# RWKV in a four-layer trunk: keys, values and gates each projected in one piece, where keys and values went by halves

## The chip, the cores and the metric

The kernel runs on one core of a Trainium2 chip. The time is device time in microseconds (us) for one execution; the kernel before took 2302.71 us, the median of 3 runs (2301.54 to 2303.0). The profile shows one such execution by the hardware profiler, with TensorE as PE (its weight loads as PEld), VectorE as DVE, ScalarE as ACT, GpSimd as POOL and SyncE as SP.

## What is computed

A trunk of four residual layers on 256 tokens of 2048 channels. Layers 0 and 3 are RWKV time mixing, layer 1 is dilated attention, layer 2 is causal pooling. Only RWKV is touched by the change:

```python
xx = jnp.pad(h, ((0, 0), (1, 0), (0, 0)))[:, :S] - h
r, k, v, g = [(h + xx * mu[j]) @ w_in[j] for j in range(4)]
...
y = _rwkv7_scan(r, decay, k, v, -kk, kk * a)       # 32 heads of 64 channels
y = (group_norm(y) + bonus) * jax.nn.silu(g)
x = x + y @ w_out
```

Each of the four projections has its own mixed input `h + xx * mu[j]`, and each is a product of [256, 2048] with [2048, 2048]. In layer 3 the values are also blended with those of layer 0 by a low-rank sigmoid.

## The kernel before

**Projections.** `linear` forms a product by blocks of 256 output columns, each with 4 weight tiles of 512 rows. float32 is split into two parts (`whi`, `wlo` of the weights by L192 on ACT and L193 on DVE; `xhi`, `xlo` of the input by L169 and L170), and three matmuls stand for one product, all on L289. A block is 96 matmuls of 128x256. A matrix of 2048 columns has 8 blocks. I count blocks from the start of the program, 150 in all: in layer 0 the receptances are blocks 0 to 7, keys, values and gates 8 to 31, and the output projection 32 to 39. In layer 3 the same stand at 110 to 117, 118 to 141, and 142 to 149.

**Mixed inputs.** `mix` (L465) makes two of the 16 tiles of `h + xx * mu`: two loads `hl` of 256 KB from DRAM on SP's queue (L474) and two DVE operations (L478); `split` then adds one ACT and one DVE operation. The 8 pairs are made once per call of `part`, by `mixer_inputs`, and kept in SBUF while that call runs.

**Heads.** `heads` does the delta rule for one pair of channel tiles (four heads, 8 pairs per layer), beside the projections. Its stages are: decay, rate and normalized key, then scores (L723); an inverse of small blocks, stage D, whose matrices go through DRAM (`ntd`, `pxd`) around 30 short DVE operations (L765, L768), with `PX` (L782) and the products `q`, `zp`, `pp` on PE behind it (L791 to L816); stage C, four chunks of 64 tokens in a chain, `xps` (L842), `X` (L846), `ups` (L849), `UV` (L852, L853), `sps` (L857), the state `SV` (L860, L862), and the outputs `yps` (L867, L870); and stage E, the norm of the heads (`gps`, L882), the bonus (`bps`), the product with the gate (L898) and a store to `zd` (L899). The output projection reads `zd` back as `zl` (L407) and splits it. Stage C needs the centred values of its pair, which `take_v` stores (`vps` L592, `vcd`) when their block is done; D and C hold one pair each at a time, and at most three pairs are in flight (`FLY`).

**What sets the order.** `order` (L227) lists the calls of `part`. While `linear` emits a block, `tick` emits the steps of the heads that fall due, and a scheduler then fixes the order of the instructions on each engine. That order is static, and each engine runs its own in order. `drain` emits what is left of the heads after the last gate; the scheduler may still set matmuls of the output projection between them, as far as its inputs `zd` are there. Two PSUM tiles `lin` and three buffers of `whi` bound how far that goes: blocks 32 and 33 can each run up to the last two of their 16 input tiles before the last pair is done.

Of the kernel before, what the change touches and what calls it, by code (L numbers as in the profile page):

```python
# [16 lines left out]
D = 2048  # L17
# [12 lines left out]
ZMIN = -40.0  # L30
# [62 lines left out]
class Trunk:  # L93
# [68 lines left out]

    # ---------------------------------------------------------------- splits
    def split(self, src):
        """The two float32r parts of a pair of [128, 256] float32 tiles."""
        nc = self.nc
        hi = self.xp.tile([P, 2, S], F32R, tag="xhi", name="xhi", bufs=9)
        lo = self.xp.tile([P, 2, S], F32R, tag="xlo", name="xlo", bufs=9)
        nc.scalar.copy(hi, src)  # L169
        nc.vector.tensor_tensor(lo, src, hi.bitcast(F32), op=ALU.subtract)  # L170
        return hi, lo

    @staticmethod
    def once(make):
        """xs(k): the parts of tile k, made in pairs when first asked for."""
        made = {}

        def xs(k):
            if k // 2 not in made:
                made[k // 2] = make(k // 2 * 2)  # L180
            hi, lo = made[k // 2]
            return hi[:, k % 2], lo[:, k % 2]

        return xs
# [11 lines left out]
    def tick(self, us):  # L196
        """Trace the work beside the projections that falls due while these take `us` of TensorE.

        Its generators yield (TensorE time, delay of the next step) or (stage, condition)."""
        self.now += us  # L200
        self.load = max(0.0, self.load - us * self.RATE)
        slack = 0.0
        while True:
# [10 lines left out]
            it = min(due, key=lambda o: (o[1] != "C", o[3]))  # L214
# [7 lines left out]
            else:  # L222
# [3 lines left out]

    order = ((1, 0, D // 2, 1), (2, 0, D // 2, 2), (1, D // 2, D, 1), (2, D // 2, D, 1),  # L227
             (3, 0, D, 2))

# [10 lines left out]
    def linear(self, wv, n_lo, n_hi, xs, consume, kt=KT, tok_major=False, rounds=0,  # L240
               wide=False, then=None, blocks=None):
        """x @ w in columns n_lo..n_hi: out^T by 128 columns, or out by 256 columns.

        blocks: the first columns of blocks of 256, in place of n_lo..n_hi.
        then: (weights, first column, x, whole) of the next call, whose first tiles are made
        ahead; with whole, all the tiles of x during the last column."""
        nc = self.nc
# [53 lines left out]

    # ------------------------------------------------------------------ norm
    def sigmoid(self, out, z, bias=None, scale=1.0):
        """out = 1 / (1 + exp(-max(scale z + bias, ZMIN))), with exp and ln alone.

        bias: a column that holds the bias less ZMIN."""
        nc = self.nc
# [4 lines left out]
    def square(self, x, first, last, direct=False):  # L312
        """Adds a pair of tiles of x^T to the sums of squares of the tokens."""
        nc, sp = self.nc, self.sp
# [34 lines left out]
    def token_scales(self):  # L349
        """The norm's factors of the tokens along a row, and along a column the factors and  # L350
        eps over their squares."""
        nc = self.nc
# [15 lines left out]
    def norm(self, layer, xt):  # L368
        """h^T of a layer, one zero column ahead of it, from the pairs of tiles of x^T."""
        nc = self.nc  # L370
# [16 lines left out]
    def spill(self):  # L387
        """h^T and its token shift's difference to DRAM, for the later projections."""
        nc = self.nc
# [13 lines left out]
    def stored(self, li):  # L403
        """Split tiles of z^T from DRAM."""
        def load(k):
# [6 lines left out]
    def out_proj(self, wv, xs, kt, li):  # L412
        """x += z @ w_out, then the next layer's norm (or the output)."""
        nc = self.nc
# [47 lines left out]

    # ------------------------------------------------------------------ RWKV
    def mix(self, l, m, k):
        """Two tiles of h + (its token shift - h) mu_m."""  # L465
        nc = self.nc
# [34 lines left out]
    def lora_in(self, l, n, pool, w2, srcs):  # L501
        """The inner activations of the low-rank maps, [rank, 256] each, step by step."""
        nc, a = self.nc, self.i
# [29 lines left out]
    def lora_out(self, out, w2, j, src, rank, key):  # L533
        """max(w0 + src @ w2, ZMIN) - ZMIN of two tiles of 128 channels."""
        nc = self.nc
# [19 lines left out]
    def rwkv(self, l, li):  # L555
# [17 lines left out]
        def take_v(j, ps):  # L573
# [13 lines left out]
            def turn():  # L587
                # centred values by token, columns (head of a tile, tile, channel)
                vps = self.ps.tile([P, 2, 2, 2, C], F32, tag="ch", name="vps", bufs=2)
# [58 lines left out]
    def heads(self, l, li, pr, w2, srcs, have):  # L648
        """Four heads (two tiles of 128 channels) of the delta rule, from k^T to the normed output."""
        nc, sp = self.nc, self.sp  # L650
# [5 lines left out]
        j = 2 * pr  # L656
        # ---- decay, in-context rate
        sg = T("sg", [P, 4, S], 1)
# [18 lines left out]
        nc.vector.tensor_copy(Wc, W[:, :, :, C])  # L677
        # ---- normalized key, key of the state
        kk = T("kk", [P, 2, S], 1)
# [34 lines left out]
        yield "S", lambda: True  # L714
        # ---- scores
        mk = self.cst("smask")
        NT = T("NT", [P, 8, C], 2)
        MR = T("MR", [64, 2, 2, NC_, C], FLY)
        for q in range(2):
# [16 lines left out]
            yield 0.0, 1.0  # L736
        # ---- keys by token
        BT = T("BT", [P, 2, NC_, P], FLY)
# [6 lines left out]
        yield 0.9, 1.0  # L745
        # ---- (1 - N)^-1 of the diagonal blocks of 16, one block in a partition
        yield "D", lambda: True
# [29 lines left out]
        yield 0.0, 14.0  # L777
        # ---- blocks of 32, then 64
        rowm = self.cst("rows")
# [45 lines left out]
        yield "C", lambda: j in have[2]  # L825
        # ---- centred values by token
        UV = T("UV", [P, NC_, 2, 2, C], 1)
# [6 lines left out]
        for hh, rows in enumerate(half):  # L834
            nc.vector.memset(SV[rows, 0, hh], 0.0)
        # ---- chunks
        Y = T("Y", [P, 2, S], 1)
        each = [(q, hh, rows) for q in range(2) for hh, rows in enumerate(half)]
        for c in range(NC_):
# [33 lines left out]
            nc.scalar.copy(Y[:, :, c * C:(c + 1) * C], yps)  # L873
        # ---- norm of a head (its values have no mean), bonus
        yield "E", lambda: True
# [27 lines left out]

    # ------------------------------------------------------------- attention
    def rope_tables(self):
# [38 lines left out]
    def attention(self, li):  # L944
# [10 lines left out]
        nc.vector.memset(qkw[0:2 * ROPE_HALF], 1.0)  # L955
        # rope tables with the norm's weights in them: x1*c, x2*s, x1*s, x2*c
        tab = T("tab", [P, 6, 4, 2, ROPE_HALF], 1)
# [72 lines left out]
    def qk_heads(self, part, g, ps, tab):  # L1030
        """Norm and rotation of two heads of queries or keys."""
        nc, sp = self.nc, self.sp
# [26 lines left out]
    def attend(self, hd, ho, qkv, mask, oT):  # L1059
        """One head's softmax over the keys of all the dilations, step by step."""  # L1060
        nc, sp = self.nc, self.sp
# [49 lines left out]

    # --------------------------------------------------------------- pooling
    def pooling(self, li):
# [109 lines left out]
def host_layout(inputs):  # L1223
    g = {k: np.ascontiguousarray(v) for k, v in inputs.items()}
    arr = {n: g[n] for n in _PLAIN}
    for n in _BLOCKS:
        # blocks of 512 rows and 256 columns, each in one piece
        w = g[n]
# [51 lines left out]
```

## Time and profile before

| | |
|---|---|
| median of 3 runs | 2302.71 us |
| span of the profiled execution | 2307.1 us |
| PE busy / weight loads busy | 97% / 92% |
| DVE / ACT busy | 69% / 56% |
| blocks 8 to 33 of layer 0 (keys to the tail of the heads) | 133.3 to 638.3 us |
| blocks 118 to 143 of layer 3 (the same) | 1694.4 to 2233.9 us |

Matmuls overlap, so a busy PE may still wait: a wait shorter than one matmul's 0.28 us doesn't show as idle. The granted clock of PE has two levels, 2.4 GHz (1.00) and 1.2 GHz (0.50).

### The profile page before, as it was taken

What the parts mean: (1) busy time and instruction counts of PE and PEld (TensorE: products, weight loads), DVE (VectorE), ACT (ScalarE), POOL (GpSimd) and SP (SyncE); (2) the same over time, 40 slices, a digit from 0 to 9 for tenths busy, and PEclk for the clock granted to TensorE, in tenths of its full rate; (3) what the DMA queues carried; (4) which work ended last, traced back from release to release, by engine and by line L of the source; (5) the groups of instructions that cost most, each with busy time, mean ns of one, the idle gap of its engine ahead of it and who ended that gap; (6) DMA issues with size and microseconds to landing.
All of it is one profiled execution on the core that took longest, in us unless ns stands there. A gap on an engine that the chain in (4) does not pass through costs nothing.

```text
span 2307.1 us, 54751 instructions
## 1 busy us (share of the span) xinstructions
PE 2234.1 (97%) x22762; PEld 2119.4 (92%) x22762; DVE 1586.6 (69%) x2965; ACT 1301.4 (56%) x2074; POOL 4.7 (0%) x12
## 2 busy tenths in 40 slices
PE   7999999999999999999999999999999999999999
PEld 6998888889899999999999999998988888888889
DVE  7678788886556555555557675657678788887654
ACT  6557666665545444444456445546657666666542
POOL 0000000000000000000000000000000000000000
PEclk9999999999999999999999999999999999999999
DMA  7686777756576655454547567776586676665665
GB/s 265 226 259 187 236 212 214 230 155 187 197 249 189 179 151 175 151 177 149 179 150 251 177 183 220 246 220 227 177 282 188 205 230 191 203 194 170 198 212 159
DMA packets 217656, 464.38 MB, mean 201 GB/s; under 512 B 55488, under 2 KB 85824, under 8 KB 217408
## 3 DMA queue, kind: packets, MB, share of 16 engines
q1 hardware_dynamic: 199264, 432.92, 60.7%
q10 hardware_dynamic: 17504, 25.87, 3.2%
q8 instruction: 178, 2.92, 0.5%
q0 software_dynamic: 640, 2.10, 0.2%
q14 instruction: 70, 0.57, 0.1%
HBM read 410.47 MB, written 50.33 MB: 200 GB/s over the span
## 4 chain that ended last, share of the span: by engine, by line
PE 79%; DVE 11%; DMA 6%; ACT 3%; issue 2%; SPq 0%; DVEq 0%; POOL 0%; ACTq 0%; POOLq 0%
PE lin L289 65%; DVE wlo L193 3%; DMA hl<-hd 2%; PE u L515 1%; ACT whi L192 1%; PE yps L870 1%; PE ups L849 1%; DVE xlo L170 1%; PE xps L842 1%; PE q L791 1%; DMA kt<-kd 1%; PE sps L857 1%; PE z L540 1%; PE sc L723 1%; PE op L1106 1%
## 5 line engine op out<-in xcount | busy, mean ns | idle before, releaser
L289 PE MATMUL lin<-xhi,whi 128*128 128x256 f32 x3584 | 1057.5, 296 | 13.4 <-ACT xhi L169 13.2
L289 PE MATMUL lin<-xlo,whi 128*128 128x256 f32 x3584 | 1026.1, 287 | 8.3 <-DVE xlo L170 8.2
L193 DVE TENSOR_TENSOR wlo<-raw,whi 128x1024 fp32r<-128x1024 f32 x600 | 732.3, 1222 | 426.9 <-ACT whi L192 416.0
L289 PE MATMUL lin<-xhi,wlo 128*128 128x256 f32 x3584 | 1023.6, 286 | 0.7 <-DVE wlo L193 0.6
L192 ACT CAST whi<-raw 128x1024 fp32r<-128x1024 f32 x600 | 626.8, 1046 | 543.7 <-PE lin L289 500.1
L289 PEld LDWEIGHTS lin<-xhi,whi 128*128 128x128 f32 x3584 | 691.0, 193 | 36.9 <-ACT xhi L169 16.2
L289 PEld LDWEIGHTS lin<-xlo,whi 128*128 128x128 f32 x3584 | 692.5, 193 | 20.0 <-DVE xlo L170 11.5
L289 PEld LDWEIGHTS lin<-xhi,wlo 128*128 128x128 f32 x3584 | 691.9, 193 | 5.0 <-issue 1.9
L289 PE MATMUL lin<-whi,xhi 128*128 128x256 f32 x1152 | 332.4, 289 | 0.0
L289 PE MATMUL lin<-whi,xlo 128*128 128x256 f32 x1152 | 325.9, 283 | 0.0
L289 PE MATMUL lin<-wlo,xhi 128*128 128x256 f32 x1152 | 325.8, 283 | 0.0
L289 PEld LDWEIGHTS lin<-wlo,xhi 128*128 128x128 f32 x1152 | 221.0, 192 | 0.2
L289 PEld LDWEIGHTS lin<-whi,xhi 128*128 128x128 f32 x1152 | 220.9, 192 | 0.2
L289 PEld LDWEIGHTS lin<-whi,xlo 128*128 128x128 f32 x1152 | 220.8, 192 | 0.0
L478 DVE SCALAR_TENSOR_TENSOR mt<-hl,prm 128x256 f32<-128x256 f32 x152 | 71.2, 476 | 31.9 <-DMA hl<-hd 31.1
L169 ACT CAST xhi<-mt 128x512 fp32r<-128x512 f32 x96 | 58.8, 616 | 44.9 <-DVE mt L478 38.6
L170 DVE TENSOR_TENSOR xlo<-mt,xhi 128x512 fp32r<-128x512 f32 x96 | 65.2, 683 | 5.0 <-ACT xhi L169 4.5
L482 ACT ACTIVATE mt<-H,omm 128x256 f32<-128x256 f32 x120 | 54.2, 501 | 20.8 <-PE u L515 11.2
L484 DVE SCALAR_TENSOR_TENSOR mt<-H,prm,mt 128x256 f32<-128x256 f32 x120 | 52.8, 480 | 15.5 <-ACT mt L482 13.9
L765 DVE TENSOR_TENSOR tmp<-px,Nb 64x15 f32<-64x15 f32 (+7 forms) x240 | 46.7, 194 | 5.8 <-DMA Nb<-ntd 1.2
L768 DVE TENSOR_TENSOR px<-px,tmp 64x15 f32<-64x15 f32 (+7 forms) x240 | 46.8, 195 | 4.5
L723 PE MATMUL sc<-AR,BK 64*128 64x128 f32 x512 | 46.0, 295 | 0.5 <-DVE tmp L765 0.3
(229 smaller groups left out, 2231.6 us busy)
## 6 DMA issues: line engine op xcount, KB each, us to landing
raw<-in_a_w_in_dram SPq DMA_DIRECT2D x256, 512.0 KB, 4.3
raw<-in_b_w_in_dram SPq DMA_DIRECT2D x160, 512.0 KB, 3.5
hl<-hd SPq DMA_DIRECT2D x152, 256.0 KB, 4.5
raw<-in_a_w_out_dram SPq DMA_DIRECT2D x64, 512.0 KB, 4.2
raw<-in_c_w_in_dram SPq DMA_DIRECT2D x64, 512.0 KB, 3.6
raw<-in_c_w_out_dram SPq DMA_DIRECT2D x32, 512.0 KB, 4.2
raw<-in_b_w_out_dram SPq DMA_DIRECT2D x16, 512.0 KB, 4.7
zl<-zd SPq DMA_DIRECT2D x24, 256.0 KB, 4.2
```

What stands on the lines that cost most here:

```text
L169: nc.scalar.copy(hi, src)
L170: nc.vector.tensor_tensor(lo, src, hi.bitcast(F32), op=ALU.subtract)
L192: nc.scalar.copy(whi, raw)
L193: nc.vector.tensor_tensor(wlo, raw, whi.bitcast(F32), op=ALU.subtract)
L289: nc.tensor.matmul(ps[:, m], a, b, start=(k == 0 and m == 0 and q == 0), stop=(k == kt - 1 and q == 2), skip_group_check=True)
L478: nc.vector.scalar_tensor_tensor(t[:, q], h[q][:, 1], mu, h[q][:, 0], op0=ALU.mult, op1=ALU.add)
L482: nc.scalar.activation(t[:, q], self.H[:, k + q, 1:], AF.Copy, scale=self.omm[:, o:o + 1])
L484: nc.vector.scalar_tensor_tensor(t[:, q], self.H[:, k + q, 0:S], mu, t[:, q], op0=ALU.mult, op1=ALU.add)
L515: nc.tensor.matmul(u[:, tt], x[:, q, tt * P:(tt + 1) * P], wt[:, k + q], start=(k + q + tt == 0), stop=(k + q == KT - 1), skip_group_check ...
L723: nc.tensor.matmul(scs[hh][:, c], BK[rows, q, c], AR[rows, hh, q, c], start=True, stop=True)
L765: nc.vector.tensor_tensor(t, px[:, 0:i + 1, 0, i:i + 1].broadcast_to([64, i + 1, w]), Nb[:, i:i + 1, i + 1:].broadcast_to([64, i + 1, w]), ...
L768: nc.vector.tensor_tensor(dst, dst, t, op=ALU.add)
```

## The change

Keys are projected in one call of 8 blocks, then values in one, then gates. Before, the calls were keys 0 to 1023, values 0 to 1023, keys 1024 to 2047, values 1024 to 2047, gates. The last number of an entry, the rounds, is not read by `linear`. As each call makes its mixed input anew, there are now three mixings per RWKV layer in place of five. Apart from this the diff drops comments and docstrings only.

```diff
-    order = ((1, 0, D // 2, 1), (2, 0, D // 2, 2), (1, D // 2, D, 1), (2, D // 2, D, 1),
-             (3, 0, D, 2))
+    order = ((1, 0, D, 1), (2, 0, D, 2), (3, 0, D, 2))
```

The same instructions stand in another order. On PE, the first chunk of each pair of layer 0 stood before at blocks 14.1, 16.8, 19.2, 21.6, 24.1, 26.6, 28.8 and 31.4, and stands now at 17.6, 19.8, 22.3, 24.9, 27.4, 29.9, 32.0 and 32.9.

PE in layer 0 before, block 32.7 of the program, where the last pair's `gps` and `bps` stand (`lin` is a product of the output projection, `xhi_8553` an input tile of an earlier pair):

```order
L289 MATMUL lin_8702<-xhi_8509,wlo_8706 128x256
L289 MATMUL lin_8702<-xhi_8553,whi_8735 128x256
L289 MATMUL lin_8702<-xlo_8554,whi_8735 128x256
L289 MATMUL lin_8702<-xhi_8553,wlo_8736 128x256
L882 MATMUL gps_8683<-gsq_8679,c1_149 128x512
L884 MATMUL bps_8685<-kp_6683,c1_149 128x512
L289 MATMUL lin_8702<-xhi_8553,whi_8735 128x256
L289 MATMUL lin_8702<-xlo_8554,whi_8735 128x256
```

PE in layer 0 now, at block 33.75, the same place (line numbers are one less; `xhi_8625` is the last pair's own input tile, read back from DRAM):

```order
L841 MATMUL xps_8434<-SV_8361,AR_6949 64x64 x4
L848 MATMUL ups_8441<-X_8439,P_8355 64x64 x4
L856 MATMUL sps_8448<-UV_8360,BT_7578 64x64 x4
L866 MATMUL yps_8457<-AR_6949,SV_8361 64x64 x4
L869 MATMUL yps_8457<-MR_7339,UV_8360 64x64 x4
L841 MATMUL xps_8467<-SV_8361,AR_6949 64x64 x4
L848 MATMUL ups_8474<-X_8472,P_8355 64x64 x4
L866 MATMUL yps_8481<-AR_6949,SV_8361 64x64 x4
L869 MATMUL yps_8481<-MR_7339,UV_8360 64x64 x4
L881 MATMUL gps_8495<-gsq_8491,c1_149 128x512
L883 MATMUL bps_8497<-kp_6880,c1_149 128x512
L288 MATMUL lin_8514<-xhi_8625,whi_8547 128x256
```

Before, 93 matmuls of `lin` stood between `bps` and the first that reads the last pair's tile; now none does, and the last two chunks have none between their steps either (in layer 3: the last one).

DVE in layer 0 before, at block 12.5, where values began (`mt` is a mixed tile of the values' input, `tmp` and `px` belong to stage D of pair 0):

```order
L765 TENSOR_TENSOR tmp_2398<-px_2215,Nb_2210 64x15
L193 TENSOR_TENSOR wlo_2318<-raw_2315,whi_2317 128x1024
L768 TENSOR_TENSOR px_2215<-px_2215,tmp_2398 64x15
L170 TENSOR_TENSOR xlo_2360<-mt_2352,xhi_2359 128x512
L765 TENSOR_TENSOR tmp_2398<-px_2215,Nb_2210 64x28
L478 SCALAR_TENSOR_TENSOR mt_2381<-hl_2382,prm_151 128x256
L768 TENSOR_TENSOR px_2215<-px_2215,tmp_2398 64x2x14
L478 SCALAR_TENSOR_TENSOR mt_2381<-hl_2384,prm_151 128x256
```

DVE now at the same place, where keys go on with the input they have:

```order
L764 TENSOR_TENSOR tmp_2354<-px_2215,Nb_2210 64x15
L193 TENSOR_TENSOR wlo_2250<-raw_2247,whi_2249 128x1024
L767 TENSOR_TENSOR px_2215<-px_2215,tmp_2354 64x15
L193 TENSOR_TENSOR wlo_2296<-raw_2293,whi_2295 128x1024
L764 TENSOR_TENSOR tmp_2354<-px_2215,Nb_2210 64x28
L728 TENSOR_TENSOR MR_2278<-sc_2279,c1_149 64x256
L767 TENSOR_TENSOR px_2215<-px_2215,tmp_2354 64x2x14
L731 TENSOR_TENSOR AR_2198<-sc_2279,c1_149 64x512
```

The mixed tiles are gone from there, and the heads' own operations follow each other.

## Rows read from the trace of the kernel before

**Rows 1.** Busy time of the page: us, share of the span, instructions.

```profile
PE 2234.1 (97%) x22762; PEld 2119.4 (92%) x22762; DVE 1586.6 (69%) x2965; ACT 1301.4 (56%) x2074; POOL 4.7 (0%) x12
```

**Rows 2.** Stretches: from:to, length, busy (count) by engine, PEclk, DMA share, GB/s.

```profile
133.30:194.30 61.00, 57.24 (x447) 54.32 (x446) 45.08 (x68) 42.64 (x64) 0.00 (x0) 0.97 0.72 231
194.30:307.40 113.10, 102.97 (x1339) 91.68 (x1337) 94.98 (x226) 70.69 (x125) 0.00 (x0) 0.95 0.74 229
307.40:606.10 298.70, 294.72 (x4186) 261.63 (x4184) 235.93 (x556) 195.68 (x357) 0.00 (x0) 1.00 0.65 197
...
1757.60:1881.30 123.70, 113.81 (x1331) 99.72 (x1331) 100.45 (x231) 78.27 (x139) 0.00 (x0) 0.92 0.70 217
1881.30:2196.30 315.00, 303.50 (x4187) 267.66 (x4186) 245.19 (x571) 204.24 (x371) 0.00 (x0) 0.98 0.63 192
```

**Rows 3.** Stretches again, L289 alone on PE, at each level of the clock.

```profile
649.80:695.90 46.10, 46.10 (x387) 46.10 (x386) 1.00 0.71 220
...
1578.90:1582.30 3.40, 3.33 (x15) 3.33 (x16) 0.50 0.99 332
```

**Rows 4.** Page's groups of mixing: count | busy us, mean ns; and its loads.

```profile
L478 DVE SCALAR_TENSOR_TENSOR mt<-hl,prm 128x256 f32<-128x256 f32 x152 | 71.2, 476 | 31.9 <-DMA hl<-hd 31.1
L170 DVE TENSOR_TENSOR xlo<-mt,xhi 128x512 fp32r<-128x512 f32 x96 | 65.2, 683 | 5.0 <-ACT xhi L169 4.5
...
hl<-hd SPq DMA_DIRECT2D x152, 256.0 KB, 4.5
```

**Rows 5.** Waits of PE, blocks 12 to 16 and 122 to 126: us, times, longest.

```profile
PE lin L289 <- DVE xlo L170: 2.9, 4, 1.5
...
PE lin L289 <- DVE xlo L170: 3.4, 4, 1.3
PE xps L842 <- DMA SV<-vcd: 3.1, 1, 3.1
PE lin L289 <- ACT xhi L169: 1.8, 3, 0.9
```

**Rows 6.** Timeline, last pair of layer 0: start, length, engine, line, operation.

```profile
621.98 1.04 PE L882 MATMUL gps<-gsq,c 128*128 128x512 f32 x2
623.31 0.68 PE L289 MATMUL lin<-xhi,whi 128*128 128x256 f32 x1
...
626.96 0.33 SPq L899 DMA_DIRECT2D zd<-Y  x1
...
632.47 0.62 ACT L169 CAST xhi<-zl 128x512 fp32r<-128x512 f32 x1 [0.81 <-DMA zl<-zd]
...
633.14 0.51 PE L289 MATMUL lin<-xhi,whi 128*128 128x256 f32 x2 [0.29 <-ACT xhi L169]
```

**Rows 7.** Timeline, last pair of layer 3, the same ends.

```profile
2217.60 1.04 PE L882 MATMUL gps<-gsq,c 128*128 128x512 f32 x2
...
2230.46 0.50 PE L289 MATMUL lin<-xhi,whi 128*128 128x256 f32 x2 [1.13 <-ACT xhi L169]
```

**Rows 8.** Timeline, steps of a chunk in layer 0's last pair.

```profile
595.22 0.45 PE L842 MATMUL xps<-SV,AR 128*64 128x64 f32 x8
595.72 0.27 ACT L846 COPY X<-xps 128x128 f32<-128x128 f32 x1 [0.69 <-PE xps L842]
...
614.29 0.39 PE L857 MATMUL sps<-UV,BT 128*64 128x64 f32 x5
615.41 0.60 DVE L862 TENSOR_TENSOR SV<-SV,Wc 64x128 f32<-64x128 f32 x2
618.07 0.45 PE L849 MATMUL ups<-X,P 64*64 64x64 f32 x8
618.95 0.26 ACT L853 COPY UV<-ups 64x128 f32<-64x128 f32 x1 [1.44 <-DVE UV L852]
```

**Rows 9.** Timeline, stage D of layer 0's last pair, from its last DVE step on.

```profile
552.77 0.18 DVE L768 TENSOR_TENSOR px<-px,tmp 64x15 f32<-64x15 f32 x1
...
566.37 0.91 ACT L782 ACTIVATE PX<-pc,c 128x256 f32<-128x256 f32 x2
```

## The prediction

> **What bounds the kernel now.** I read the page's busy times first. PE is busy 97% of the span and its weight loads 92%, DVE 69% [rows 1], so outside of short places the time is PE's work. The change leaves PE the same instructions. So the question is only where PE waits, and at which clock it works, before and after. Next I read a quiet stretch of L289 alone: four blocks, 384 matmuls, in 46.1 us, that is 0.12 us for one; with the granted clock at 0.50, 15 to 16 in 3.40 us, some 0.21 us [rows 3]. Time at the low level thus loses 1 - 0.12/0.21 = 0.44 of itself.
>
> Then I cut layer 0's scan by blocks, and layer 3's like it [rows 2]. The reader is to take length less PE's busy time as its idle time, and twice (1 less the granted clock) times the length as time at the low level.
> - Blocks 12 to 16 (values by their first half, start of the second half of keys): layer 0, 113.1 us, idle 10.1, low level 11.3 us, so 5.0 lost by it. Blocks 122 to 126 in layer 3: 123.7 us, idle 9.9, low level 19.8, so 8.7 lost. Together 33.7 us in ten blocks.
> - Blocks 17 to 31, and 127 to 141: 298.7 and 315.0 us, idle 4.0 and 11.5, low level about 0 and 12.6 (5.5 lost). 21 us in thirty blocks.
> - Blocks 8 to 11 have keys with stage A of two pairs, and are the same after: 61.0 us, idle 3.8.
>
> So the waits are densest where the halves change over. The waits there have names [rows 5]: PE on the split input tiles, 2.9 in layer 0 and 3.4 + 1.8 in layer 3, is 8.1 us of mixing itself; the 3.1 us on SV is the heads' own.
>
> Last I read the end of the scan, since the heads end later now. In layer 0 the last pair's `gps` starts at 621.98, its result is stored at 626.96, its tile read back is split at 632.47, and the first matmul that reads it starts at 633.14: 11.2 us. In layer 3 it is 2217.60 to 2230.46: 12.9 us. PE waited only 0.29 and 1.13 us of that, as 93 matmuls of the output projection (11.2 us) stood between [rows 6, 7].
>
> **The change part by part.**
>
> *Two mixings less per layer.* For each, 8 pairs with two DVE operations of 0.476 and one of 0.683, 13.1 us; two of them in two layers are 52 us of DVE, and 64 loads of 256 KB less on SP's queue [rows 4]. None of that is PE's time; it pays only as waits that go. Floor: the 8.1 us by name. Ceiling in those ten blocks: all 33.7. In the new order four of the five blocks hold keys alone, since the heads stop at three pairs in flight until values come; I expect them to wait like blocks 8 to 11 do, some 4 us per layer, so 33.7 - 8 = 26 us gained. The heads' work that is no longer there isn't gained, it is moved behind.
>
> *Blocks 17 to 33.* One mixing (for gates) stands there still, in place of three; values' own is made in block 16. But the stages C and E of all pairs lie there now, and SV's load comes 36 projection matmuls after `vps`, so layer 0 may wait on it as layer 3 did (3.1). The named waits on mixing there are near nothing, so I take a gain of 2 us in both layers, with ends of -10 (the idle time per block as now, over two more blocks, and the SV wait twice) and +10 (half of the 21).
>
> *The end of the heads.* In the order, no matmul of the output projection is left between `bps` and the first that reads the last pair's tile, in either layer: blocks 32 and 33 have run to their 14th input tile. So the way from `gps` to that tile is bare: 11.2 and 12.9 less some 1.3 us for `gps` and `bps` themselves (621.98 to 623.31), less the 0.29 and 1.13 waited already: 20.1 us in both layers [rows 6, 7]. Ends: 18 and 24, since the two layers differ by 1.7 us already.
>
> *The last chunks, bare.* From `xps` to the end of X 0.77 us, from `ups` to the end of UV 1.14, from `sps` to the end of SV 1.72: 3.6 us, in which PE works 5 steps of 0.45, so 1.4 us of waiting per chunk without cover [rows 8]. The last chunk has no `sps`, so 0.6, and then the copy of Y and its square, 1.1 us. I take 3 us per layer, 6; ends 3 and 10.
>
> *Stage D of the last pair.* From its last DVE step to the start of PX passed 13.4 us (552.95 to 566.37), then 0.9 for PX [rows 9], all behind projections. In the new order some 57 projection matmuls (6.9 us) and two chunks and the norm of pair 6 (about 5 us by the steps of rows 8 and the 1.3 of `gps` and `bps`) stand between that step and the first product `q`. So about 2 us is bare, and some 1 us in the products behind it, which have few projections between them. 3 us per layer, 6; ends 0 and 28 (all of it bare).
>
> *The clock.* The stretch at 1578.90, at 0.50, stands where layer 3 begins, behind the norm that PE waits for [rows 3]. A bare end of 10 us and a sparse PE ahead of it should do the same, for one to two such stretches: 0.44 of 3.4 to 10 us, 1.5 to 4.5 per layer. I take 3, so 6.
>
> *More changes between kinds of matmul.* PE's order goes from `lin` to something else 171 and 189 times in the two scans, 157 and 178 before. Where a small matmul follows `lin`, the start comes some 0.1 us later than another `lin` would, and going back costs as much: 25 times 0.2 us is 5 at most; I take 4.
>
> Sum: -26 - 2 + 20 + 6 + 6 + 6 + 4 = +14 us. The profiled span is 2307.1 us, so 2321 on that scale; it lies 4.4 above the median, 2302.71, which gives 2317.
>
> On whether less DVE work pays at all, stretch and span differ: over the span DVE is far behind PE, yet in blocks 12 to 16 it is busy 95.0 of 113.1 us, and the weight loads 91.7 [rows 1, 2]. The Trainium skill (Perfetto Trace Analysis, Identifying the Most-Contended Engine) says to optimize the engine with the highest occupancy first, with the weight loads as PE's measure. Read over the whole span it gives the 26 + 2 us no place; read by stretch it lets DVE count there.
>
> **The rivals.**
>
> *Faster: waits fall by more than I count, from stage to stage.* Waits shorter than 0.28 us don't show as idle, and each one that is removed also spares time at the low clock. If all 33.7 us and another 10 of the middle go, against the low ends at the tail (18 + 3 + 0 + 3 + 2 = 26), the sum is -18: 2285; I put the middle of this case at -12, 2291. It decides from the point where the ten blocks give back more than the 42 us that I charge the end. For it: 52 us of DVE time and 16.8 MB of loads are really gone. Against it: only 8.1 us of PE's waits bear the name of mixing.
>
> *No change.* The same gain meets a cheaper end; within 5 us either side of 2303.
>
> *Much slower: the last pair's stage D is bare.* If its round trip through DRAM isn't covered, 14 us per layer stand in place of 3: +22, 2339. It decides from the point where pair 6's chunks end before the inverse is back. For it: in layer 3 fewer projections (48) stand before `q`. Against it: DMA is busy 0.65 of the time in the middle [rows 2] and will have less to move.
>
> *DVE's relief gives nothing.* PE is the bound in every stretch, so the gain is 0 and the end costs its 42: 2345. The waits on `xlo` and `xhi` speak against it [rows 5]. The rule of the Trainium skill named above (Perfetto Trace Analysis, Identifying the Most-Contended Engine), read over the whole span, is this case.
>
> *The change doesn't do what it says:* the order shows that it does, in both layers.
>
> **How the numbers follow.** Forecast 2317, with its own range 2308 to 2330 from the ends of the single terms: 0.50. Faster, at 2291: 0.20. No change: 0.13. Stage D bare: 0.11. No relief: 0.06. A difference under 0.2%, 4.6 us, can't be told from none. The forecast's share lies above that, so slower is 0.50 + 0.11 + 0.06 = 0.67, same 0.13, faster 0.20. The range of 8 in 10 goes from 2293, inside the faster case, to 2341, past the bare stage D.
>
> **What would show it.** In the new profile: PE idle for 9 to 13 us in each RWKV layer right before the first L288 that reads the last pair's tile, released by ACT L169 after `zl`, and the granted clock at 0.50 behind it; blocks 12 to 16 shorter by far, some 70 us, with the granted clock near 1.00 and no named wait on `xlo`; L477 88 times in place of 152; the blocks from 17 on longer. If PE waits at the end for less than 5 us, the step on the bare way is wrong; if blocks 12 to 16 still hold 10 us of idle time, the step on mixing is. If the middle shows 20 us more or less idle time than now, the whole sum is wrong in its sign or its size.

## The result: 2.4% slower, four times the forecast's loss

| us | before | after |
|---|---|---|
| median beside each other (4 runs each) | 2302.86 | 2360.41 (2353.61 to 2369.87) |
| ratio, 95% interval | | 1.024 (1.0208 to 1.0271) |
| the profiled execution's span | 2307.1 | 2351.7 |
| time at the low level of TensorE's clock in it | 68 | 117 |
| the changed kernel again, on another chip | 2308.70 | 2357.39, 1.0191 (1.0153 to 1.0229) |

The forecast was 2317, from 2293 to 2341. The sign was right, the size was not: 43 us are missing, and the time lies outside the range.

The page of the changed kernel: busy time by engine, beside [rows 1], and its group and loads of mixing, beside [rows 4]:

```profile
PE 2265.1 (96%) x22762; PEld 2136.3 (91%) x22762; DVE 1547.3 (66%) x2869; ACT 1287.5 (55%) x2042; POOL 4.7 (0%) x12
...
L477 DVE SCALAR_TENSOR_TENSOR mt<-hl,prm 128x256 f32<-128x256 f32 x88 | 41.0, 480 | 23.5 <-DMA hl<-hd 23.3
...
hl<-hd SPq DMA_DIRECT2D x88, 256.0 KB, 4.7
```

The relief is there as announced: PE has the same 22762 matmuls, DVE 96 operations and SP 64 loads less. Yet PE's busy time is 31 us longer. No matmul was added, so what grew is the time of some of them. The clock was at its low level 49 us longer; at the prediction's price of 0.44 that is some 22 of the 31 us. Where the other 9 come from is not shown.

The scans by blocks, as in [rows 2] (length, busy time and count of PE, PEld, DVE, ACT, POOL, granted clock, DMA share, GB/s). The rows of each layer are blocks 8 to 11, 12 to 16, 17 to 31, and 32 and 33; in layer 3 the same from 118 on:

```profile
132.70:194.20 61.50, 57.59 (x446) 54.25 (x445) 45.11 (x68) 41.87 (x62) 0.00 (x0) 0.97 0.70 227
194.20:270.60 76.40, 70.55 (x789) 67.36 (x788) 58.55 (x130) 44.52 (x67) 0.00 (x0) 0.98 0.66 214
270.60:590.00 319.40, 314.39 (x4277) 275.10 (x4275) 237.79 (x544) 206.29 (x374) 0.00 (x0) 0.99 0.60 181
590.00:668.30 78.30, 63.07 (x755) 49.69 (x754) 33.16 (x91) 26.24 (x54) 0.00 (x0) 0.80 0.38 124
1724.30:1788.10 63.80, 58.69 (x447) 55.15 (x446) 45.46 (x68) 41.94 (x62) 0.00 (x0) 0.95 0.69 218
1788.10:1864.00 75.90, 72.15 (x793) 68.08 (x791) 59.02 (x130) 45.96 (x71) 0.00 (x0) 0.98 0.68 216
1864.00:2204.50 340.50, 331.37 (x4305) 287.02 (x4303) 253.19 (x573) 222.25 (x404) 0.00 (x0) 0.96 0.60 178
2204.50:2278.50 74.00, 61.21 (x754) 49.25 (x753) 33.43 (x86) 25.10 (x52) 0.00 (x0) 0.86 0.38 125
```

And the same two last rows of the kernel before, which do not stand ahead of the prediction:

```profile
606.10:638.30 32.20, 31.91 (x297) 28.52 (x294) 19.19 (x32) 17.44 (x30) 0.00 (x0) 1.00 0.60 205
2196.30:2233.90 37.60, 36.25 (x334) 31.21 (x333) 19.42 (x35) 17.17 (x29) 0.00 (x0) 1.00 0.53 182
```

Blocks 12 to 16 are shorter by 37 and 48 us, but they also hold some 550 matmuls less. Most of those stand in blocks 32 and 33 now (755 in place of 297, 754 in place of 334), which are longer by 46 and 36 us and hold 28 us of idle time at a clock of 0.80 and 0.86. Outside the two scans the two executions agree: span less the scans is 1262.6 us before and 1261.9 after. So the 44.6 us lie in the scans.

With the prediction's two measures (idle time, and 0.44 of the time at the low level) these rows give:

| part, both layers, us | before | after | difference | forecast |
|---|---|---|---|---|
| blocks 12 to 16: idle + clock | 20.0 + 13.7 | 9.6 + 2.7 | -21 | -26 |
| blocks 17 to 31: idle + clock | 15.5 + 5.5 | 14.1 + 14.8 | +8 | -2 |
| blocks 32 and 33: idle + clock | 1.6 + 0 | 28.0 + 22.9 | +49 | +38 |
| the rest of 44.6, not told apart (forecast: changes between kinds of matmul) | | | +9 | +4 |

The end of layer 0's scan in the changed kernel, line by line, beside [rows 6], and the same matmuls of layer 3, beside [rows 7] (start, length, engine, line, operation, idle time before it and its releaser):

```profile
651.43 2.08 PE L881 MATMUL gps<-gsq,c 128*128 128x512 f32 x2 [1.01 <-ACT gsq L877]
653.30 1.91 PE L883 MATMUL bps<-kp,c 128*128 128x512 f32 x2
...
658.31 0.33 SPq L898 DMA_DIRECT2D zd<-Y  x1
...
662.99 0.62 ACT L169 CAST xhi<-zl 128x512 fp32r<-128x512 f32 x1 [8.10 <-DMA zl<-zd]
...
663.66 0.80 PE L288 MATMUL lin<-xhi,whi 128*128 128x256 f32 x2 [8.44 <-ACT xhi L169]
...
2262.64 1.12 PE L881 MATMUL gps<-gsq,c 128*128 128x512 f32 x2 [1.02 <-ACT gsq L877]
...
2273.26 0.79 PE L288 MATMUL lin<-xhi,whi 128*128 128x256 f32 x2 [8.63 <-ACT xhi L169]
```

The way from `gps` to the last tile takes 12.2 and 10.6 us, and PE stands idle for 8.4 and 8.6 of them: the bare end is where the prediction put it. What it did not see is around it. Layer 0's tail in pieces:

```profile
616.00:626.00 10.00, 6.01 (x246) 5.12 (x246) 4.19 (x7) 3.57 (x6) 0.00 (x0) 1.00 0.56 186
626.00:640.00 14.00, 14.00 (x125) 11.66 (x120) 3.62 (x9) 3.48 (x8) 0.00 (x0) 0.51 0.13 40
640.00:650.00 10.00, 8.22 (x117) 6.37 (x113) 4.28 (x12) 2.90 (x8) 0.00 (x0) 1.00 0.18 55
650.00:667.00 17.00, 7.54 (x24) 4.52 (x23) 3.65 (x7) 2.91 (x6) 0.00 (x0) 0.50 0.31 93
```

From 626 to 640 PE has no idle time at all, and yet its granted clock is 0.51: it fell at 626.0, behind ten microseconds in which PE worked 6.0. It is low a second time from 650 to 667. That is 31 us at the low level in one tail, and 51 in both layers together.

### The profile page after: what moved, and what is told of

It is laid out like the page before. It is cut to its first block, busy times and chain, and to the rows that moved or that the text cites. A ratio compares the mean times of both kernels' runs of the same rounds, so it can differ in the third digit from the quotient of the medians.

```text
span 2351.7 us, 54546 instructions
## 1 busy us (share of the span) xinstructions
PE 2265.1 (96%) x22762; PEld 2136.3 (91%) x22762; DVE 1547.3 (66%) x2869; ACT 1287.5 (55%) x2042; POOL 4.7 (0%) x12
## 5 line engine op out<-in xcount | busy, mean ns | idle before, releaser
L481 ACT ACTIVATE mt<-H,omm 128x256 f32<-128x256 f32 x120 | 54.1, 501 | 20.5 <-PE u L514 12.1
L851 DVE COPY UV<-ups 64x128 f32<-64x128 f32 x64 | 18.0, 281 | 61.6 <-PE ups L848 60.7
L169 ACT CAST xhi<-mt 128x512 fp32r<-128x512 f32 x64 | 39.4, 616 | 33.1 <-DVE mt L477 27.4
L477 DVE SCALAR_TENSOR_TENSOR mt<-hl,prm 128x256 f32<-128x256 f32 x88 | 41.0, 480 | 23.5 <-DMA hl<-hd 23.3
L859 DVE TENSOR_TENSOR SV<-SV,sps 64x128 f32<-64x128 f32 x96 | 27.3, 284 | 33.4 <-PE sps L856 31.6
```

What stands on the lines that cost most here:

```text
L477: nc.vector.scalar_tensor_tensor(t[:, q], h[q][:, 1], mu, h[q][:, 0], op0=ALU.mult, op1=ALU.add)
L481: nc.scalar.activation(t[:, q], self.H[:, k + q, 1:], AF.Copy, scale=self.omm[:, o:o + 1])
L859: nc.vector.tensor_tensor(SV[rows, c + 1, hh], SV[rows, c, hh], sps[rows], op=ALU.add)
```

## The experiments

All ratios are to the kernel before, run on the same chip in the same comparison (medians 2307.5, 2308.7, 2307.8 and 2307.2 us). Differences in us are the ratio's.

### Is it mixing? Three mixings in the old order, five in the new

`three`: the order by halves, but the second halves make no new mixed input (the second half of the keys is computed from the values' one).

```diff
-                    then = (win(m2), lo2, self.mixer_inputs(l, m2), False)
+                    then = (win(m2), lo2, xs if n in (1, 2) else self.mixer_inputs(l, m2), False)
```

> The order of before, but only three mixings per RWKV layer: the second halves of keys and of values are projected from the mixed input that the first half of the values made (so the second half of the keys is computed from the wrong mixed input; the count and order of the projections are before's, 64 loads of 256 KB and 52 us of DVE are gone). If the mixings themselves were what PE waited for in blocks 12 to 16 (theory: mixing), the time falls by 20 to 30 us against before, to some 2275 to 2283. If those waits were the heads' own, which only moved (rival: heads), it falls by less than 8, to 2295 to 2303.

Measured: 2294.86 us, 0.994 (0.9917 to 0.9962), -13 us. Its blocks 12 to 16 and 122 to 126, beside the second and fourth line of [rows 2]:

```profile
196.20:305.20 109.00, 101.75 (x1338) 90.70 (x1336) 89.85 (x223) 67.70 (x118) 0.00 (x0) 0.97 0.68 208
...
1755.50:1874.50 119.00, 111.55 (x1331) 97.99 (x1330) 95.80 (x233) 74.93 (x133) 0.00 (x0) 0.93 0.64 200
```

With the heads left where they were, two mixings less per layer shorten these stretches by 4.1 and 4.7 us, not by 13 each as the forecast's 26 would have it. Idle time there is 14.7 us in place of 20.0. This does not show that the other waits are the heads' own, for the two mixings don't lie wholly in these blocks: of the 55 operations L478 that the kernel before has in the ten blocks, `three` keeps 32, and waits on split input tiles of 5.4 us, of 8.1, are left. What the run does bound is the worth of both mixings over the whole kernel, 13 us.

`remix`: the new order with five mixings (keys and values in two calls each, at the same places).

```diff
-    order = ((1, 0, D, 1), (2, 0, D, 2), (3, 0, D, 2))
+    order = ((1, 0, D // 2, 1), (1, D // 2, D, 1), (2, 0, D // 2, 2), (2, D // 2, D, 1),
+             (3, 0, D, 2))
```

> The changed order (all keys, all values, gates), but with five mixings as before: the calls are keys 0 to 1023, keys 1024 to 2047, values 0 to 1023, values 1024 to 2047, gates, so each half makes its input anew. PE's order is that of the changed kernel. Theory mixing: 20 to 26 us slower than the changed kernel, 2380 to 2386. Rival heads: blocks 12 to 16 are so light now that the two mixings are covered, 0 to 8 us slower, 2360 to 2368.

Measured: 2372.26 us, 1.0294 (1.0242 to 1.0347), +68. That is 12 us above the changed kernel's 1.024, and 24 above its 1.0191; the intervals overlap in the first case. The mixings are thus worth 13 us in the old order and 12 or 24 in the new one, by the first or the second time of the changed kernel; moving the projections alone costs 68.

### Is it the bare end? Cut it short, fill it, or make one in the old order

`direct`: the changed kernel, with the last pair's gated output kept in SBUF, without its store and load.

```diff
-            dma(self.zd[li % 2][j // 2], Y)
+            if j == KT - 2:
+                self.zlast = self.mp.tile([P, 2, S], F32, tag="mt", name="zlast", bufs=2)
...
+            if k == KT - 2 and self.zlast is not None:
+                t, self.zlast = self.zlast, None
+                return self.split(t)
```

> The changed kernel, but the last pair's gated output stays in SBUF and is split from there; its store to DRAM and the load of it back are left out, nothing else. Theory: the end of the heads is bare, so what is taken from its chain comes off the time: store and load were 5.5 us in layer 0 and 7 in layer 3 before, so 11 to 13 us faster than the changed kernel, 2347 to 2350, and some of the time at the low clock with it. Rival (something else ends last there, or the loss lies in the middle): within 4 us of 2360.

Measured: 2355.23 us, 1.0214 (1.018 to 1.0248). Less than the 11 to 13 us expected, and not told apart from the changed kernel's 1.024 and 1.0191. PE's longest wait at the end of layer 0 in it (lines are one or more further, by the edit), and the stretch:

```profile
PE lin L289 <- ACT xhi L170: 3.7, 1, 3.7
```

```profile
597.30:674.40 77.10, 66.18 (x757) 52.53 (x754) 33.81 (x90) 26.55 (x54) 0.00 (x0) 0.78 0.36 120
```

The wait fell from 8.4 to 3.7 us, yet the two blocks take 77.1 us in place of 78.3: the clock there is 0.78 in place of 0.80, so 3 us more at the low level. Taking away the wait did not take away what surrounds it. From the last `gps` to the end of the scan pass 11.9 and 12.1 us in place of 15.9 and 15.3, so some 7 us in both layers were saved there; a gain of that size lies within the intervals, and the run can neither show nor exclude it.

`dummy`: the changed kernel with eight useless 128x512 matmuls put into that wait.

```diff
+        if j == KT - 2:
+            dps = self.ps.tile([P, 2, S], F32, tag="ch", name="dps", bufs=2)
+            for _ in range(8):
+                nc.tensor.matmul(fl(dps), self.cst("bd"), fl(sq), start=True, stop=True)
```

> The changed kernel with useless work added: eight matmuls of 128x512 into a spare PSUM tile, from the last pair's reciprocal norms, in the bare wait at the end of each RWKV layer's heads (some 7 us of PE that would idle). Theory clock: the granted clock is at 0.50 when the projection goes on because PE idled, so the useless work makes the kernel 2 to 6 us faster, and the low stretch behind the wait is gone from the clock's records. Rival: the low clock there comes from the sparse chunks ahead or costs nothing: within 2 us, or up to 2 us slower.

Measured: 2358.74 us, 1.0211 (1.0184 to 1.0238), again the changed kernel's time. PE's idle time at the end of layer 0 falls to 7.8 us, but the clock was already low when the filling began:

```profile
595.10:676.40 81.30, 73.53 (x771) 55.55 (x770) 32.91 (x89) 26.11 (x54) 0.00 (x0) 0.79 0.35 118
...
631.30:665.20 33.90, 31.67 (x245) 24.00 (x242) 8.86 (x23) 8.58 (x20) 0.00 (x0) 0.50 0.11 33
665.40:676.40 11.00, 9.64 (x40) 5.52 (x39) 3.47 (x8) 1.88 (x3) 0.00 (x0) 1.00 0.44 143
```

The useless matmuls start at 664.1, so the low level was there before the wait that they fill. Behind them it is gone: the clock is high again from 665.3 on, where the changed kernel's projection still ran at 0.50 for some 3 us behind its wait (663.7 to 667). Neither shows in the time of the whole kernel, so the run does not separate the wait from the clock.

`bare`: the kernel before, but the RWKV output projections read their input tiles from the last to the first, so that nothing covers the heads' end. One index stayed as it was, so a tile meets another tile's weights of its group of four; number, shape and order of instructions are as described.

```diff
+            kcs = list(range(kt // 4))[::-1 if rev else 1]
...
+                k = kc * 4 + (3 - k4 if rev else k4)
...
+        self.linear(wv, 0, D, xs, consume, kt=kt, then=then, rev=self.layers[li] % 3 == 0)
```

> The kernel before, five mixings and its order of columns; only the output projections of the two RWKV layers read their sixteen input tiles from the last to the first, so that none of their matmuls can stand before the last pair of heads is done. Nothing of the heads or of mixing changes, nothing is left out. Theory end (what the change costs is that the heads' last steps lose the output projection's matmuls that covered them): in the kernel before, from the start of the output projection to the first matmul on the last pair's tile pass 27 us in layer 0 (606.1 to 633.1) and 34 in layer 3 (2196.3 to 2230.5), during which some 15 to 17 us of heads' matmuls stand; PE waits the rest, 10 to 17 us per layer, later steps lose their cover as well, and the low level follows: +25 to +55 us, ratio 1.011 to 1.024. Rival (the end costs little, as the heads run faster with PE to themselves, and the loss of the change comes from the middle): 0 to +10 us, ratio at most 1.004. The low level's time rises from 68 to over 100 us by the first, stays under 80 by the rival.

Measured: 2342.02 us, 1.0131 (1.0103 to 1.016), +30, inside the first theory's range. PE's wait for the last tile in layer 0 and in layer 3 (the projection is L292 here), and blocks 17 to 31 of layer 0, which end with it:

```profile
PE lin L292 <- ACT xhi L169: 8.6, 1, 8.6
...
PE lin L292 <- ACT xhi L169: 8.5, 1, 8.5
```

```profile
311.90:636.60 324.70, 306.78 (x4286) 268.98 (x4284) 244.64 (x576) 204.34 (x375) 0.00 (x0) 0.97 0.63 192
```

The waits themselves are those of the changed kernel (8.4 and 8.6). The time at the low level rose from 68 to 106 us, and 0.44 of that rise is 17 us: about as much as the 17 us of named waits.

`direct_b`: the edit of `direct` in the kernel before.

> The kernel before, only the last pair's gated output stays in SBUF and is split from there, without its store and load. If the way from the last gps to its tile is covered in the kernel before by the output projection's matmuls (PE waited 0.29 and 1.13 us there): 0 to -2 us, ratio 0.999 to 1.000. Rival (the end of the scan hangs on the heads there too, since it follows the last gps by 16 us before and after alike): -6 to -10 us, ratio 0.9955 to 0.9975.

Measured: 2305.95 us, 0.9989 (0.9973 to 1.0005). No gain beyond the 2 us expected: in the kernel before that way is covered, as [rows 6, 7] were read.

### Is it the heads' later start?

`late`: the kernel before with its order by halves and its five mixings; only the first pair's chunks wait for the first keys of the second half.

```diff
-        yield "C", lambda: j in have[2]
+        yield "C", lambda: j in have[2] and (pr or 8 in have[1])
```

> The kernel before with its order by halves and its five mixings; only the chunks of the first pair of heads wait until the first keys of the second half are there, so that the first xps stands at block 17.06 and 126.94 (14.1 and 124.1 in the kernel before, 17.6 and 127.75 after the change) and the last gps at 33.75 and 143.75, as after the change. Nothing is left out. Theory start (the heads are a chain of eight pairs, 340 to 355 us from the first gps to the last in every kernel so far, and the scan's end follows the last gps by 16 us; what the change costs is that this chain starts about three blocks later): as the changed kernel with five mixings, first gps some 36 us later in the scan, +40 to +60 us, ratio 1.017 to 1.026. Rival (the loss comes from whole columns, from the order of the projections, not from the heads' start): below +15 us, ratio at most 1.0065.

Measured: 2371.84 us, 1.028 (1.026 to 1.0299), +65: slightly above the range, and with five mixings the same as `remix`. No projection was moved here. The first `xps` of layer 0 (operation, count, length, first and last start) in the kernel before, the changed kernel and `late`; below them the end stretches of `late`:

```profile
L842 PE MATMUL xps<-SV,AR x8: 314/314/369, 246.2 to 246.6; 128*64 128x64 f32 x8
```

```profile
L841 PE MATMUL xps<-SV,AR x8: 222/314/369, 284.2 to 286.0; 128*64 128x64 f32 x8
```

```profile
L842 PE MATMUL xps<-SV,AR x24: 222/222/270, 286.9 to 307.6; 128*64 128x64 f32 x24
```

```profile
604.30:684.10 79.80, 66.54 (x756) 52.76 (x753) 35.01 (x95) 25.76 (x54) 0.00 (x0) 0.76 0.38 121
...
2223.20:2301.70 78.50, 66.44 (x755) 52.85 (x754) 33.69 (x88) 25.15 (x53) 0.00 (x0) 0.76 0.38 121
```

Its end is much like the changed kernel's: 79.8 and 78.5 us, 25 us idle, a clock of 0.76. In all these kernels the heads are a chain of eight pairs of about the same length. Read from the starts of `xps` and `gps` in the traces (the last `gps` by its last matmul), in us from the start of each scan (layer 0 / layer 3):

| kernel | first xps | first gps | last gps | end of block 33 / 143 |
|---|---|---|---|---|
| before | 113 / 117 | 148 / 159 | 489 / 524 | 505 / 540 |
| three | 115 / 116 | 151 / 158 | 489 / 512 | 505 / 528 |
| o1280 | 127 / 122 | 158 / 159 | 508 / 514 | 523 / 530 |
| six | 128 / 133 | 167 / 163 | 512 / 519 | 527 / 538 |
| after | 152 / 157 | 184 / 196 | 520 / 539 | 536 / 554 |
| again (the changed kernel) | 155 / 154 | 190 / 189 | 530 / 530 | 547 / 545 |
| late | 154 / 157 | 196 / 198 | 535 / 544 | 552 / 561 |
| remix | 161 / 165 | 195 / 207 | 536 / 563 | 552 / 579 |

From the first `gps` to the last pass 336 to 365 us in every row, and the scan ends 15 to 18 us behind the last. From before to after a start that is 36 us later in layer 0 gives an end that is 31 us later. In layer 3 37 us at the start give 14 at the end: there the chain of the kernel before took the longest of all, 365 us, and that of the changed kernel took 343. In `again` it is 42 us that give 41 in layer 0, and 30 that give 5 in layer 3. So the chain's shift goes over to the end almost whole in layer 0, and in layer 3 only in part; why the chain of layer 3 is so long before the change stays open.

`six`: a dose between the two, keys of six pairs, all values, the other keys, gates (four mixings).

```diff
+    order = ((1, 0, 1536, 1), (2, 0, D, 2), (1, 1536, D, 1), (3, 0, D, 2))
```

> A dose between the two kernels: keys of six pairs of tiles (1536 columns), all values, the keys' last 512 columns, gates; four mixings. The first products xps stand at block 15.5 (14.1 in the kernel before, 17.6 after the change), the last gps at 33.15 and 143.1 (32.8 and 142.9 before, 33.75 after). Theory end: of the 11 to 13 us from gps to the last tile 57 and 62 matmuls of the output projection (7 us) remain as cover, so 4 to 6 us are bare per layer in place of about 10 after the change: +10 us, with 3 to 6 us of low level, less one mixing of the two that gave 12 in the order before (-6): +2 to +10 us, ratio 1.001 to 1.004. Rival (the loss is that values and the chunks start late at all, or it comes whenever the order isn't by halves): half or more of the change's 50 us, ratio 1.010 or over.

Measured: 2330.36 us, 1.009 (1.006 to 1.0121), +21: over the first theory's range and just under the second's. The sign of the dose is right. The first theory, which counts only the bare way at the end, is too low again.

`again`: the changed kernel beside these.

> The changed kernel once more, beside these on one chip: ratio 1.021 to 1.027 as measured, with 110 to 130 us at the low level in its profile; the share of the end blocks (32, 33, 142, 143) in the loss as before, 45 to 55 us. If the low level's time and the end's waits vary from run to run while the rest stays, the spread of the changed kernel's times belongs to them.

Measured: 2357.39 us, 1.0191 (1.0153 to 1.0229), just under the 1.021 to 1.027 expected, with an interval that overlaps the first one's; 107 us at the low level, just under the 110 to 130 expected. Its end blocks take 81.5 and 73.8 us, its blocks 12 to 16 76.0 and 74.8. The forecast's miss is no accident of one execution.

### Four mixings, with the heads nearly in place

`o1280`: as `six`, with five pairs of keys first. This was to keep half of the mixing's gain without the later end.

```diff
+    order = ((1, 0, 1280, 1), (2, 0, D, 2), (1, 1280, D, 1), (3, 0, D, 2))
```

> Keys of five pairs of tiles (1280 columns), all values, the keys' last 768 columns, gates: four mixings, while the first xps stands at block 14.75 and the last gps at 32.90 and 142.90, nearly as in the kernel before (14.1; 32.78 and 142.90). Theory end with mixing: one mixing less without a later end gives half of the 12 us that two gave, less 1 to 3 us for the 11 matmuls less of cover in layer 0: -6 to -2 us, ratio 0.9975 to 0.999. Rival (mixing's relief pays only where the order by halves stays): 0 to +8 us, ratio 1.000 to 1.0035.

Measured: 2320.14 us, 1.0055 (1.003 to 1.008), +13. Both expectations missed. The trace shows, in layer 0, a late sixth pair of heads, whose keys come only with the second part: its `gps` at 430 us of the scan in place of 407. The two after it follow, and the scan ends 18 us later. In layer 3 of this one execution it ends 10 us earlier.

`fb2` and `oc`: the kernel before and `o1280` with one number of the planner changed, so that heads' steps are put in earlier.

```diff
-    CAP = 1.0
+    CAP = 2.0
```

> The kernel before with one number of the planner changed: heads' steps other than chunks may be put in while up to 2.0 us of such work lies unhidden (1.0 before). The first xps stands at 13.9 (14.1) and the last gps at 32.47 in layer 0 and 142.47 in layer 3 (32.78, 142.9). Theory start: heads some 0.3 block (4 us) earlier, but the matmuls between them and the end were covered already, so nothing comes back there: -5 to +5 us, ratio 0.998 to 1.002. Rival (the scan's end hangs on the last gps before the change too): -6 to -10 us, ratio 0.9955 to 0.9975.

> Keys of 1280 columns, all values, the other keys, gates, four mixings, with the planner's number at 2.0 in place of 1.0: the last gps at 32.65 and 142.65, earlier than in the order of 1280 columns alone (32.90, 142.90) and than in the kernel before (32.78, 142.90). Theory start: the 11 us by which that order lay above the kernel before came from the heads' last two pairs, 0.6 block later there; at the same place or earlier they go, and one mixing less shows: -8 to 0 us, ratio 0.9965 to 1.000. Rival (values by whole columns cost by themselves): +6 to +15 us, ratio 1.0025 to 1.0065.

Measured: `fb2` 2314.96 us, 1.0039 (1.0023 to 1.0056); `oc` 2324.8 us, 1.0087 (1.0067 to 1.0107). Both expectations of `fb2` missed: a last `gps` that is earlier in the order cost 9 us, where 5 at most was forecast, and in layer 0 it is not earlier in time: it stands at 496 us in place of 489. In `oc` the sixth pair's `gps` is at 426 us and the last at 504, 4 us before `o1280` and 15 behind the kernel before. An earlier place in the order is thus not an earlier time, and the theory's expectation of `oc` failed; the rival's range lies below the time too.

`mix0` and `mix3`: the order of `o1280` in layer 0 only, and in layer 3 only.

```diff
+            order = ((1, 0, 1280, 1), (2, 0, D, 2), (1, 1280, D, 1), (3, 0, D, 2)) if l == 0 else self.order
```

> The same order in layer 0 only; layer 3 as in the kernel before. Theory chain: in layer 0 the sixth pair of heads, whose keys come only with the keys' second part, ends its last step 23 us later in the trace (430 us from the scan's start in place of 407), and the scan ends 12 to 18 us later: +12 to +18 us, ratio 1.005 to 1.008. Rival (values by whole columns cost by themselves, in either layer): +3 to +8 us, ratio 1.001 to 1.0035, as in layer 3.

> The order with keys of 1280 columns ahead of all values (four mixings) in layer 3 only; layer 0 as in the kernel before. Theory chain (the heads' chain sets each scan's end; in layer 3 it is slowed in the kernel before by waits around blocks 122 to 141, and one mixing less eases them): layer 3's scan 525 to 531 us in place of 539.5, so -14 to -8 us, ratio 0.994 to 0.997. Rival (values by whole columns cost by themselves, in either layer): +3 to +8 us, ratio 1.001 to 1.0035.

Measured: `mix0` 2319.06 us, 1.0078 (1.0048 to 1.0108); `mix3` 2312.53 us, 1.001 (0.9986 to 1.0033). `mix0` lies in the chain's range and far above its rival's, so the loss is in layer 0, with the sixth pair's `gps` at 424 us there. In `mix3` the chain's forecast of -14 to -8 us failed. The gain of layer 3 that the trace of `o1280` seemed to show is not there: in `mix3` the scan of layer 3 takes 542.1 us in place of 539.5, with 40 us at the low level in place of 34. Why one mixing less brings nothing visible there stays open. No order that was tried beats the kernel before; `three` does, but it does not compute the same keys.

## Why the prediction was right in sign and wrong in size

**Right.** The bare way at the end: 20 us forecast for both layers beyond the 1.4 waited before; PE waits 8.4 and 8.6 for the tile, so 15.7 more. (The 1.0 twice for the square ahead of `gps` belongs to the term of the last chunks.) Stage D of the last pair is not bare by much: PE waits 2.1 and 1.9 us at `q`, where about 2 per layer were forecast, so that rival falls. The idle time forecast at the end, 32 us, was if anything high: the rows give 26 more than before. Blocks 12 to 16 have the length (76 us, some 70 forecast) and nearly the clock forecast (0.98). Idle time and clock cost 12 us there in both layers, where 8 were forecast. The named waits on mixing are gone there but for 0.6 us on `xhi`, and `L477` stands 88 times.

**Wrong: which terms.** In the profiled pair 44.6 us stand against 14 forecast. By the rows of the table, of the 31 us between, the clock at the end holds 17 (22.9 for 6), the middle 10 (+8 for -2), blocks 12 to 16 5 (-21 for -26) and the rest 5 (+9 for +4), while idle time at the end gives 6 back (26 for 32). The other 12 us of the miss lie between this pair and the medians.

**Wrong, the clock.** The step "3 per layer, so 6" took the low level to be one or two stretches of 3.4 to 10 us. Blocks 32 and 33 alone hold about 31 and 20 us of it, 22.9 us lost; the middle loses 9 more than before. The price of 0.44 itself nearly holds: two executions of the changed kernel, spans 2351.7 at a clock of 0.976 and 2368.0 at 0.967, differ by 16.3 us for 42 us more at the low level (twice 0.009 times the span), 0.38 each. The median lies 7 us above the profiled execution for that reason.

**Wrong, the gain in blocks 12 to 16.** The text itself says that work which is no longer there "isn't gained, it is moved behind", and then counted the whole fall of the waits, 26 us, as gained, with -2 for the blocks behind. `three` shows the mixing's part in the old order: 13 us over the whole kernel. The floor of 8.1 us by named waits was nearer to it than the 26 that were chosen. Blocks 17 to 31 stand at +8 in place of -2, all of it clock (14.8 for 5.5): idle time there fell by 1.4. Two waits there are the ones the text named, PE on the load of SV:

```profile
PE xps L841 <- DMA SV<-vcd: 2.6, 1, 2.6
...
PE xps L841 <- DMA SV<-vcd: 2.5, 1, 2.5
```

**What the sum lacked.** It priced the end as three pieces without cover. `late` shows the whole: the heads' chain starts 39 to 48 us later by its first `gps` (36 and 37 in the changed kernel), and that alone costs 65 us in two layers with five mixings; two mixings less give 13 back, and 52 is within the 44 to 55 us of the changed kernel. How much of the 65 is wait and how much is clock is not divided by it. A rival on these lines (the start of the chain, its 341 and 365 us and the 16 behind it, all readable before) was not among the five.

**The other rivals.** "DVE's relief gives nothing" is refuted by `three`, where taking only DVE and ACT work and loads away gained 13 us, with the weight loads at 92% of the span and DVE at 69%. The Trainium skill (Perfetto Trace Analysis, Identifying the Most-Contended Engine) says to optimize the engine with the highest occupancy first. Read over the whole span it would have given that gain no place, so the measurement sides with the reading by stretch. "Faster" needed more than 42 us from the ten blocks; they gave 21.

**Still open.** How the end's loss divides between waits and clock is known from the traces' records alone: in `direct` and `dummy` PE's idle time there is 18.8 and 13.1 us in place of 28.0 (in `dummy` because useless work fills it), and neither shows in the time. Open too are the 9 us of the rest, and why layer 3 answers to the chain's start so much less than layer 0.

## What to carry to other kernels

Where a serial chain runs beside the bound engine and ends with it, first ask when the chain starts: a later start moves its end too (by 31 of 36 us in layer 0 and by 14 of 37 in layer 3 here), and work that covered the end cannot be used twice. Count waits that leave a stretch as moved until the waits by name say that they are gone; here the named floor, 8 us, was nearer to the 13 measured in the old order than the 26 read off the stretch. Price an end without cover twice, once for the waits and once for the clock over the whole sparse stretch.

## What was not expected of the hardware

The granted clock was at 0.51 for 14 us in which PE had no idle time on record, from 626 to 640, after ten microseconds in which it worked 6.0; filling the later wait with matmuls (`dummy`) left the end at 0.79, with 34 us on end at 0.50 in which PE had only 2.2 us of idle time. And time at the low level differs between executions of one kernel: the ten of `o1280` range from 2309.67 us at a mean clock of 0.989 to 2335.96 at 0.981. A difference of some 10 us can't be read from one profile of each kernel, as layer 3 of `o1280` and `mix3` showed.
